# First mixer of a two-layer decoder trunk: tap rows and block sums move into the buffers of x, and twelve of thirty taps go by DMA

## The chip, the cores and the metric

The kernel runs on one core of one Trainium2 chip. The metric is the device time of one execution in microseconds; three executions of the kernel before took 2146.83, 2148.3 and 2149.0 us, median 2148.3.

## What is computed

The reference is a two-layer trunk on a sequence of 1024 positions with 1024 channels. Layer 0 is the part that the change touches:

```python
def even_mixer(h, w_in, sc_conv_w, cf_conv_w, cf_conv_b, cf_ln_g, cf_ln_b, w_out):
    z = h @ w_in
    sc_b, sc_c, sc_x, cf_a, cf_g = jnp.split(
        z, [SC_WIDTH, 2 * SC_WIDTH, 3 * SC_WIDTH, 3 * SC_WIDTH + CF_WIDTH], axis=-1)
    y_sc = sc_b * causal_dwconv(sc_c * sc_x, sc_conv_w)
    u = cf_a * jax.nn.sigmoid(cf_g)
    u = causal_dwconv(u, cf_conv_w) + cf_conv_b
    u = jax.nn.silu(layernorm(u, cf_ln_g, cf_ln_b))
    return jnp.concatenate([y_sc, u], axis=-1) @ w_out
...
        h = rmsnorm(x, mix_norm_g[layer])
        if layer % 2 == 0:
            x = x + even_mixer(h, ev_w_in[j], ev_sc_conv_w[j], ev_cf_conv_w[j], ev_cf_conv_b[j],
                               ev_cf_ln_g[j], ev_cf_ln_b[j], ev_w_out[j])
```

The Conformer convolution (cf) has 31 taps over 512 channels, the short convolution (sc) three. Each layer ends in a gated feed-forward block. Inputs and outputs are float32.

## The kernel before

Everything is held transposed: channels on the 128 partitions, the 1024 positions along the row. A tile of 128 x 1024 is one block of 128 channels; 512 channels are four blocks, j = 0 to 3. Each float32 operand of a matmul is split into a high and a low part, so a product of 1024 x 128 weights with the normalised input is 48 matmuls of 128 x 512 (`in_unit`, all issued at L229).

The first mixer (`mixer0`) runs twenty such products: for each cf block a value and a gate (pa0, pg0, pa1, ... pg3), then for each sc block three (pc, px, pb). A weight tile comes from HBM by `fetch` (L167, SP's queue, two buffers) and is split into its parts by a cast on ACT (L179) and a subtraction on DVE (L180). Products go to PSUM tiles `mm`, of which there are three, and DVE reads them out: for cf blocks L734 and L737 in `cf_evac`, with a sigmoid on ACT (L735) between them; for sc blocks L789, L793 and L800. A product starts when its weights are split and one of the three `mm` buffers has been read out.

In `cf_evac` the gated block is t and the convolution's sum u starts on ACT with the last tap and the bias (L739). The other 30 taps per block are of two kinds. Those in `taps` are one DVE instruction each, u += w * shifted t (L743, taps 10 to 30). Those in `ptaps` (taps 1 to 9) are a scaled, shifted copy that ACT writes (L754, L757), into one buffer of the sum `box["a"]` for tap 1 and into a row of the pool `e` (7 buffers) for the others, followed by a DMA from POOL's queue that adds the row to the sum (L758). At a block's end DVE adds that sum to u (L762). `run(6, 3)` between the products emits up to three `ptaps` and six `taps`.

A scheduler of the framework reorders what is emitted by its own model of the times; the order in which the instructions stand on each engine is then fixed. Each engine works its own list off in that order and stops at the first instruction whose inputs or buffers are not ready. What matters on ACT is that the casts, the sigmoids, the first sc tap (L795) and the tap rows share one list.

After the products, eight output tiles are formed, four per half of the sequence (`out_pair`, L400 adds them to x on DVE), while sums over channels for the layernorm are taken: L819 to L821 sum the four blocks, L829 and L832 square them on ACT, L833 adds the squares on POOL. Through all of this x itself, 4 MB, is resident in four slots of the pool `xpool` (`class X`, two slots for each half of the sequence); the mixer's in-projections need only its normalised copy.

Of the kernel before, what the change touches and what calls it, by code (L numbers as in the profile page):

```python
# [12 lines left out]
AF = mybir.ActivationFunctionType  # L13
ALU = mybir.AluOpType
# [4 lines left out]
S = 1024  # L19
NT = S // P  # L20
KD = D // P
# [21 lines left out]
U_EVIN, U_EVOUT = 0, 20  # L43
# [8 lines left out]
def trunk(ctx, tc, x, wpk, par, wgate, masks, ident, out):  # L52
    nc = tc.nc
# [11 lines left out]
    def nm(s):  # L65
        uid[0] += 1
        return f"{s}_{uid[0]}"
# [4 lines left out]
    def g_tile(dt=F32):  # L72
        return E["g"].tile([P, 1024], dt, tag="g", name=nm("g"))

    def x_tile(slot, a=4, b=512):
        return xpool.tile([P, a, b], F32, tag=f"x{slot}", name=nm("x"))
# [14 lines left out]
    def e_tile(dt=F32):  # L91
        return E["e"].tile([P, 1024], dt, tag="e", name=nm("e"))

    def mm_tile():
        return E["mm"].tile([P, 1024], F32, tag="mm", name=nm("mm"))
# [69 lines left out]
    def fetch(u):  # L165
        raw = raw_tile()
        nc.sync.dma_start(raw, wpk[u])  # L167
        return raw
# [7 lines left out]
    def split(raw, alloc, parts=(slice(0, 1024),)):  # L176
        hi, lo = w_pair() if alloc is None else (alloc(), alloc())
        for p in parts:
            nc.scalar.copy(hi[:, p], raw[:, p])  # L179
            last_lo[0] = nc.vector.tensor_sub(lo[:, p], raw[:, p], hi[:, p].bitcast(F32))  # L180
        return hi, lo

    def load_w(u, alloc=None):
        raw = raws.pop(u) if u in raws else fetch(u)
        return split(raw, alloc, cuts) if u == U_EVIN else split(raw, alloc)

    xs = [X(2 * hf) for hf in range(2)]
# [7 lines left out]
    for i in range(1, 8):  # L195
        hf, c = i // 4, 2 * (i % 4)
# [10 lines left out]
    def pc(name, i=0):  # L207
        c = _C[name] + i
        return parm[:, c:c + 1]
# [18 lines left out]
    def mm(o, l, r, st, sp):  # L228
        nc.tensor.matmul(o, lhsT=l, rhs=r, start=st, stop=sp)  # L229
# [12 lines left out]
    def diag(dg, rs, nt):  # L242
        for T in range(nt):
            nc.scalar.activation(dg[:, T * P:(T + 1) * P], idt, AF.Identity, scale=rs[:, T:T + 1])
# [126 lines left out]
    def in_first(units, norm, hooks):  # L371
        pss, ws = [], []
        for hf in range(2):
            for i, u in enumerate(units):
                if hf == 0:
                    ws.append(load_w(u))
                    pss.append(mm_tile())
                in_part(pss[i], ws[i], norm.hT, hf, lambda k: hooks.get((hf, i, k), lambda: None)())
        return pss

    def in_unit(u, hT):
        w = load_w(u)
        ps = mm_tile()
        in_full(ps, w, hT)
        return ps
# [16 lines left out]
    def conv_rest(t, src, ws, n):  # L402
        for j in range(1, n):
            nc.vector.scalar_tensor_tensor(t[:, j:], src[:, :S - j], ws(n - 1 - j), t[:, j:], ALU.mult, ALU.add)  # L404
# [319 lines left out]
        st.close()  # L724


    def mixer0(xs, norm, hooks):
        hT = norm.hT
        us, taps, ptaps = [], [], []
        NPT = 9  # L730

        def cf_evac(j, pa, pg):
            sg, t = e_tile(), g_tile()
            nc.vector.tensor_mul(sg, norm.br, pg)  # L734
            nc.scalar.activation(sg, sg, AF.Sigmoid)  # L735
            nc.vector.tensor_mul(sg, sg, norm.br)
            nc.vector.tensor_mul(t, sg, pa)  # L737
            u = e_tile()
            nc.scalar.activation(u, t, AF.Identity, bias=pc("cfb", j), scale=pc("cfw", 4 * 30 + j))  # L739
            us.append(u)  # L740

            def dve(s):
                return lambda: nc.vector.scalar_tensor_tensor(  # L743
                    u[:, s:], t[:, :S - s], pc("cfw", 4 * (30 - s) + j), u[:, s:], ALU.mult, ALU.add)

            box = {}

            def pool(s):
                def f():
                    w = pc("cfw", 4 * (30 - s) + j)  # L750
                    if s == 1:
                        box["a"] = g_tile()
                        nc.vector.memset(box["a"][:, 0:1], 0.0)
                        nc.scalar.activation(box["a"][:, 1:], t[:, :S - 1], AF.Identity, scale=w)  # L754
                    else:
                        tmp = e_tile()
                        nc.scalar.activation(tmp[:, s:], t[:, :S - s], AF.Identity, scale=w)  # L757
                        nc.gpsimd.dma_start(box["a"][:, s:], tmp[:, s:], accum_op=ALU.add)  # L758
                return f
            ptaps.extend(pool(s) for s in range(1, NPT + 1))  # L760
            taps.extend(dve(s) for s in range(NPT + 1, 31))
            taps.append(lambda: nc.vector.tensor_add(u, u, box["a"]))  # L762

        def run(n, m):
            for _ in range(min(m, len(ptaps))):
                ptaps.pop(0)()
            for _ in range(min(n, len(taps))):
                taps.pop(0)()

        cf = [U_EVIN + i for i in range(8)]  # L770
        pa0, pg0, pa1 = in_first(cf[:3], norm, hooks)
        cf_evac(0, pa0, pg0)
        run(6, 3)
        pg1 = in_unit(cf[3], hT)
        cf_evac(1, pa1, pg1)
        run(6, 3)
        for j in (2, 3):
            pa = in_unit(cf[2 * j], hT)
            run(6, 3)
            pg = in_unit(cf[2 * j + 1], hT)  # L780
            cf_evac(j, pa, pg)
            run(6, 3)

        ysc = []
        for j in range(4):
            u = U_EVIN + 8 + 3 * j
            pcv = in_unit(u, hT)
            c = e_tile()
            nc.vector.tensor_mul(c, norm.br, pcv)  # L789
            nc.vector.tensor_mul(c, c, norm.br)  # L790
            run(6, 3)
            px = in_unit(u + 1, hT)
            nc.vector.tensor_mul(c, c, px)  # L793
            t = e_tile()
            nc.scalar.activation(t, c, AF.Identity, scale=pc("scw", 8 + j))  # L795
            conv_rest(t, c, lambda i: pc("scw", 4 * i + j), 3)
            nc.vector.tensor_mul(t, t, norm.br)
            run(6, 3)
            pb = in_unit(u + 2, hT)
            nc.vector.tensor_mul(t, t, pb)  # L800
            ysc.append(split(t, r_tile))
            run(6, 3)
        run(1000, 1000)


        parts = [(ysc[k], load_w(U_EVOUT + k)) for k in range(4)]

        def out_sc(i):
            out_pair(xs, i // 4, i % 4, parts)

        def colsum(on, sm):
            ps = mm_tile()
            for hf in range(2):
                s = slice(hf * 512, (hf + 1) * 512)
                mm(ps[:, s], on, sm[:, s], True, True)
            return ps

        sm = e_tile()
        nc.gpsimd.tensor_add(sm, us[0], us[1])  # L819
        nc.gpsimd.tensor_add(sm, sm, us[2])  # L820
        nc.vector.tensor_add(sm, sm, us[3])  # L821
        out_sc(0)
        pm = colsum(one1, sm)
        sq = e_tile()
        for j in range(4):
            nc.vector.scalar_tensor_tensor(us[j], pm, -1.0 / 512.0, us[j], ALU.mult, ALU.add)
        for j in range(4):
            if j == 0:
                nc.scalar.activation(sq, us[j], AF.Square)  # L829
            else:  # L830
                s2 = e_tile()
                nc.scalar.activation(s2, us[j], AF.Square)  # L832
                nc.gpsimd.tensor_add(sq, sq, s2)  # L833
        for T in (1, 2, 3):
            out_sc(T)
        rs = colvec(sq, 8, 1.0 / 512.0)
        dg = e_tile()
        diag(dg, rs, 8)
        for T in (4, 5):
            out_sc(T)  # L840
        pr = colsum(one1, dg)
        vh, vl = rows4(), rows4()
        ycf = []
        for j in range(4):
            nc.vector.tensor_mul(us[j], us[j], pr)
            nc.scalar.activation(us[j], us[j], AF.Silu, bias=pc("lnb", j), scale=pc("lng", j))
            nc.scalar.copy(vh[j], us[j])
            nc.vector.tensor_sub(vl[j], us[j], vh[j].bitcast(F32))
            ycf.append((vh[j], vl[j]))
        for T in (6, 7):  # L850
            out_sc(T)
        return [(ycf[k], load_w(U_EVOUT + 4 + k)) for k in range(4)]


    def lru(norm):
# [452 lines left out]
    norm = Plain(0, xs)  # L1308
# [6 lines left out]
    def second():  # L1315
        norm.spread(0)
        for c in range(KD):
            norm.stat(1, c)

    parts = mixer0(xs, norm, {(0, 2, 4): lambda: norm.prep(0), (1, 0, 0): second,  # L1320
                              (1, 1, 4): lambda: norm.prep(1), (1, 2, 2): lambda: norm.spread(1)})

    ste.close()
# [21 lines left out]
    box = {}  # L1345
# [18 lines left out]
    norm = box["n"]  # L1364
# [8 lines left out]
    norm, early = attention(ys, norm, st)  # L1373
# [95 lines left out]
```

## Time and profile before

| | |
|---|---|
| median of three runs | 2148.3 us |
| profiled execution, its own time | 2147.01 us |
| its span, first to last instruction | 2145.2 us |
| PE busy | 2078.2 us, 97% |
| DVE busy | 1534.0 us, 72% |
| ACT busy | 915.5 us, 43% |
| POOL busy | 218.6 us, 10% |
| mean granted TensorE clock | 0.986 of full |
| chain that ended last | PE 68%, DVE 11%, DMA 10% of the span |

The profile is of one execution. Busy time counts an engine's own instructions, not its waits; a matmul's end is modelled, so PE's idle time tells more than its busy share. The trace gives for each idle stretch what ended it ("<-"). The first mixer lies between 0 and about 320 us of the span, the cf and sc products between 6 and 254 us.

### The profile page before, as it was taken

The numbers are of one execution on the slowest core, as the hardware profiler recorded it, in microseconds if no ns is written. First come the engines' busy times: TensorE is split into PE (matmuls) and PEld (weight loads), VectorE is DVE, ScalarE is ACT, GpSimd is POOL, SyncE is SP. The second block draws the span as 40 slices with busy tenths as digits, with TensorE's granted clock in tenths as the row PEclk, the third lists the DMA queues.
The fourth block names the chain that finished last, engine by engine and source line by source line (L and its number), as shares of the span: only waits on it lengthen the run. The fifth ranks groups of instructions, "written<-read, shape, count | busy, mean of one in ns | idle before, by whom it ended". The sixth has DMA issues, their size and how long they took to land.

```text
span 2145.2 us, 26963 instructions
## 1 busy us (share of the span) xinstructions
PE 2078.2 (97%) x10260; PEld 1741.1 (81%) x10260; DVE 1534.0 (72%) x2185; ACT 915.5 (43%) x1446; POOL 218.6 (10%) x209
## 2 busy tenths in 40 slices
PE   8997998999999999998999999999899999999999
PEld 6886886888888888787889999877688888888877
DVE  6987858878788777758595233585988787776764
ACT  6433335444444333436373444453544344443332
POOL 0111200000000000000044121220000000000000
PEclk9999998999999999999999999998899999999999
DMA  4566321344434478642212211232254443469643
GB/s 175 120 140 133 88 70 69 118 133 128 116 111 133 133 229 291 215 128 99 69 40 80 90 50 43 88 96 93 68 138 133 133 123 112 120 186 313 213 146 108
DMA packets 121202, 271.75 MB, mean 127 GB/s; under 512 B 12016, under 2 KB 20720, under 8 KB 121072
## 3 DMA queue, kind: packets, MB, share of 16 engines
q1 hardware_dynamic: 106672, 235.89, 33.3%
q0 software_dynamic: 14112, 33.99, 8.9%
q8 instruction: 80, 1.31, 0.3%
q14 instruction: 50, 0.41, 0.1%
q10 hardware_dynamic: 288, 0.15, 0.0%
HBM read 174.59 MB, written 78.71 MB: 118 GB/s over the span
## 4 chain that ended last, share of the span: by engine, by line
PE 68%; DVE 11%; DMA 10%; issue 2%; ACT 2%; POOL 0%; SPq 0%; DVEq 0%; ACTq 0%; POOLq 0%
PE u L461 38%; PE pq L229 8%; PE u L636 7%; PE mm L229 7%; DMA rd<-in_wpk_dram 4%; DMA g<-e 2%; PE S L229 2%; PE pl L229 2%; PE ud L636 2%; DMA rd<-fscr 1%; DVE x L914 1%; DMA hT<-in_wpk_dram 1%; DVE w L612 1%; DVE hT L283 1%; DVE x L641 1%
## 5 line engine op out<-in xcount | busy, mean ns | idle before, releaser
L461 PE MATMUL u<-hT,s 128*128 128x512 f32 x2016 | 481.7, 391 | 1.1 <-DVE s L453 1.0
L461 PEld LDWEIGHTS u<-hT,s 128*128 128x128 f32 x2016 | 379.0, 188 | 83.1 <-DVE s L453 1.9
L229 PE MATMUL mm<-hT,w 128*128 128x512 f32 x1536 | 364.0, 397 | 24.1 <-DVE e L800 9.4
L229 PEld LDWEIGHTS mm<-hT,w 128*128 128x128 f32 x1536 | 292.6, 191 | 91.7 <-issue 18.7
L461 PE MATMUL u<-w,s 128*128 128x512 f32 x1056 | 255.6, 390 | 1.4 <-ACT x L506 1.4
L461 PEld LDWEIGHTS u<-w,s 128*128 128x128 f32 x1056 | 198.6, 188 | 44.6 <-ACT x L506 1.8
L229 PE MATMUL pq<-w,hT 128*128 128x256 f32 x1728 | 223.3, 286 | 0.7 <-ACT k L996 0.5
L229 PEld LDWEIGHTS pq<-w,hT 128*128 128x128 f32 x1728 | 211.6, 191 | 3.8 <-issue 1.3
L636 PE MATMUL u<-w,w 128*128 128x512 f32 x616 | 184.0, 393 | 4.3 <-DVE w L612 4.3
L452 ACT CAST s<-ts 128x512 fp32r<-128x512 f32 x176 | 108.7, 620 | 138.0 <-PE u L461 130.2
L453 DVE TENSOR_TENSOR s<-ts,s 128x512 fp32r<-128x512 f32 x176 | 119.4, 687 | 55.9 <-ACT s L452 55.9
L461 PE MATMUL u<-hy,s 128*128 128x512 f32 x528 | 140.1, 408 | 11.5 <-DVE s L453 6.6
L636 PEld LDWEIGHTS u<-w,w 128*128 128x128 f32 x616 | 116.0, 189 | 30.0 <-DVE w L612 5.2
L461 PEld LDWEIGHTS u<-hy,s 128*128 128x128 f32 x528 | 102.4, 195 | 37.4 <-DVE s L453 8.0
L404 DVE SCALAR_TENSOR_TENSOR x<-x,parm,x 128x1023 f32<-128x1023 f32 x88 | 112.5, 1280 | 17.3 <-ACT x L489 15.2
L636 PE MATMUL u<-w 128*128 128x512 f32 x308 | 112.3, 390 | 0.0
L611 ACT CAST w<-rd 128x1024 fp32r<-128x1024 f32 x68 | 69.6, 1048 | 86.7 <-PE u L636 72.3
L180 DVE TENSOR_TENSOR w<-raw,w 128x1024 fp32r<-128x1024 f32 (+2 forms) x61 | 77.0, 1264 | 41.1 <-ACT w L179 40.9
L743 DVE SCALAR_TENSOR_TENSOR e<-g,parm,e 128x1010 f32<-128x1010 f32 (+20 forms) x84 | 102.2, 1256 | 1.9 <-ACT e L739 1.7
L179 ACT CAST w<-raw 128x1024 fp32r<-128x1024 f32 (+2 forms) x61 | 62.5, 1031 | 82.8 <-PE mm L229 43.8
L636 PE MATMUL u<-hy,hy 128*128 128x512 f32 x328 | 97.8, 392 | 0.0
L489 ACT ACTIVATE x<-x,parm 128x1024 f32<-128x1024 f32 x44 | 54.8, 1246 | 96.0 <-DVE x L488 96.0
(254 smaller groups left out, 3080.0 us busy)
## 6 DMA issues: line engine op xcount, KB each, us to landing
raw<-in_wpk_dram SPq DMA_DIRECT2D x103, 512.0 KB, 4.1
fscr<-x SPq DMA_DIRECT2D x154, 256.0 KB, 4.2
rd<-fscr SPq DMA_DIRECT2D x58, 512.0 KB, 4.6
r<-in_wpk_dram SPq DMA_DIRECT2D x44, 512.0 KB, 4.2
fscr<-x POOLq DMA_DIRECT2D x66, 256.0 KB, 8.1
xscr<-x SPq DMA_DIRECT2D x48, 256.0 KB, 2.3
x<-xscr SPq DMA_DIRECT2D x24, 512.0 KB, 6.5
hT<-in_wpk_dram SPq DMA_DIRECT2D x22, 512.0 KB, 8.3
```

Source lines behind the costliest of these rows:

```text
L179: nc.scalar.copy(hi[:, p], raw[:, p])
L180: last_lo[0] = nc.vector.tensor_sub(lo[:, p], raw[:, p], hi[:, p].bitcast(F32))
L229: nc.tensor.matmul(o, lhsT=l, rhs=r, start=st, stop=sp)
L283: nc.vector.scalar_tensor_tensor(lo, src, scale, hi.bitcast(F32), ALU.mult, ALU.subtract)
L404: nc.vector.scalar_tensor_tensor(t[:, j:], src[:, :S - j], ws(n - 1 - j), t[:, j:], ALU.mult, ALU.add)
L452: nc.scalar.copy(w[:, 0, :], self.s[name])
L453: nc.vector.tensor_sub(w[:, 1, :], self.s[name], w[:, 0, :].bitcast(F32))
L461: nc.tensor.matmul(bank, lhsT=l, rhs=r[:, k, :], start=first and k + j == 0, stop=k == 3 and j == 2, skip_group_check=True)
L489: nc.scalar.activation(t, g, AF.Identity, bias=pc(f"fb{layer}", f), scale=pc(f"fw{layer}", 44 + f))
L611: nc.scalar.copy(hi[:, c, :], src)
L636: nc.tensor.matmul(bank[m], lhsT=l[:, w, c], rhs=r[:, b, :], start=first and j == 0, stop=j == 2, skip_group_check=True)
L743: return lambda: nc.vector.scalar_tensor_tensor(u[:, s:], t[:, :S - s], pc("cfw", 4 * (30 - s) + j), u[:, s:], ALU.mult, ALU.add)
```

## The change

x is no longer kept: once its normalised copy exists, the four slots of `xpool` are given to the tap convolution, each as two rows of 1024. Slots 0 and 1 hold tap rows in turn (four rows in all), slots 2 and 3 hold two sums per block, for odd and even taps, blocks in turn. Twelve taps per block go by DMA instead of nine: taps 1 and 2 are written directly into the two sums (L763), taps 3 to 12 are rows (L766) that are added to the sum of their parity (L767), and after tap 12 one more DMA adds one sum to the other (L769). DVE keeps taps 13 to 30 (L750) and the final add (L773). The emission is `run(5, 3)` six times and then `deal`, which spreads what is left evenly. After the last product x is loaded again by eight DMAs on POOL's queue (L825). Five adds of the layernorm's sums move from POOL to DVE.

```diff
-    def mixer0(xs, norm, hooks):
+    def mixer0(norm, hooks):
...
-        NPT = 9
+        NPT = 12
+        rows = []
+
+        def tap_row():
+            if not rows:
+                t = x_tile(len(ptaps) // 2 % 2, 2, 1024)
+                rows.extend((t[:, 1, :], t[:, 0, :]))
+            return rows.pop()
...
                     if s == 1:
-                        box["a"] = g_tile()
-                        nc.vector.memset(box["a"][:, 0:1], 0.0)
-                        nc.scalar.activation(box["a"][:, 1:], t[:, :S - 1], AF.Identity, scale=w)
+                        box["a"] = x_tile(2 + j % 2, 2, 1024)
+                    a = box["a"][:, s % 2, :]
+                    if s <= 2:
+                        nc.vector.memset(a[:, 0:s], 0.0)
+                        nc.scalar.activation(a[:, s:], t[:, :S - s], AF.Identity, scale=w)
                     else:
-                        tmp = e_tile()
+                        tmp = tap_row()
                         nc.scalar.activation(tmp[:, s:], t[:, :S - s], AF.Identity, scale=w)
-                        nc.gpsimd.dma_start(box["a"][:, s:], tmp[:, s:], accum_op=ALU.add)
+                        nc.gpsimd.dma_start(a[:, s:], tmp[:, s:], accum_op=ALU.add)
+                    if s == NPT:
+                        nc.gpsimd.dma_start(box["a"][:, 1, :], box["a"][:, 0, :], accum_op=ALU.add)
...
-            taps.append(lambda: nc.vector.tensor_add(u, u, box["a"]))
+            taps.append(lambda: nc.vector.tensor_add(u, u, box["a"][:, 1, :]))
...
+        left = [12]
+
+        def deal():
+
+            n = left[0]
+            left[0] -= 1
+            run(-(-len(taps) // n), -(-len(ptaps) // max(n - 2, 1)))
...
-        run(1000, 1000)
+        xs = [X(0), X(2)]
+        for hf in range(2):
+            for c in range(0, KD, 2):
+                nc.gpsimd.dma_start(xs[hf].c(c, 2), x[hf, :, c:c + 2, :])
...
-        nc.gpsimd.tensor_add(sm, us[0], us[1])
-        nc.gpsimd.tensor_add(sm, sm, us[2])
+        nc.vector.tensor_add(sm, us[0], us[1])
+        nc.vector.tensor_add(sm, sm, us[2])
...
-                nc.gpsimd.tensor_add(sq, sq, s2)
+                nc.vector.tensor_add(sq, sq, s2)
```

The six `run(6, 3)` of the cf part become `run(5, 3)`, the twelve of the sc part `deal()`.

How the order moves is seen at three places. The first is POOL's list at the first block's accumulations, with the semaphores that each waits for; DMASW0, DMASW1 and so on are those of POOL's DMAs, given out in turn. Before (the sum is g_54_412):

```order
L758 DMA g_54_412<-e_55_415 128x1022 [waits Activation_49]
L758 DMA g_54_412<-e_56_418 128x1021 [waits DMASW0_49,Activation_49]
L758 DMA g_54_412<-e_63_489 128x1020 [waits DMASW1_49,Activation_49]
L758 DMA g_54_412<-e_64_492 128x1019 [waits DMASW2_49,Activation_49]
L758 DMA g_54_412<-e_65_495 128x1018 [waits DMASW3_49,Activation_49]
```

And now (the tile of both sums is x_54_412):

```order
L767 DMA x_54_412<-x_55_417 128x1020 [waits Activation_49]
L767 DMA x_54_412<-x_62_489 128x1019 [waits DMASW0_49,Activation_49]
L767 DMA x_54_412<-x_62_489 128x1018 [waits DMASW1_49,Activation_49]
L767 DMA x_54_412<-x_66_553 128x1017 [waits DMASW2_49,Activation_49]
L767 DMA x_54_412<-x_66_553 128x1016 [waits DMASW3_49,Activation_49]
L767 DMA x_54_412<-x_67_558 128x1015 [waits DMASW4_49,Activation_49]
L767 DMA x_54_412<-x_67_558 128x1014 [waits DMASW5_49,Activation_49]
L767 DMA x_54_412<-x_74_630 128x1013 [waits DMASW6_49,Activation_49]
L767 DMA x_54_412<-x_74_630 128x1012 [waits DMASW7_49,Activation_49]
L769 DMA x_54_412<-x_54_412 128x1024 [waits DMASW1_49,DMASW0_49]
```

Before, the second accumulation (128x1021) waited for the first, the third for the second. Now the second on the list (128x1020, the first row shown) waits for ACT alone, the third for the first, and so on, each for the one two places ahead; the joining DMA waits for both sums.

The second place is ACT's list up to the first sc activation. Before (e_781 to e_787 are rows of block 1, e_856 and e_859 the first of block 2):

```order
L757 ACTIVATE e_93_781<-g_61_482,parm_76 128x1017
L757 ACTIVATE e_94_784<-g_61_482,parm_76 128x1016
L757 ACTIVATE e_95_787<-g_61_482,parm_76 128x1015
L179 CAST w_133_1166<-raw_132_1164 128x1024
L757 ACTIVATE e_101_856<-g_76_628,parm_76 128x1022
L757 ACTIVATE e_102_859<-g_76_628,parm_76 128x1021
L179 CAST w_141_1240<-raw_140_1238 128x1024
L795 ACTIVATE e_106_923<-e_99_850,parm_76 128x1024
```

And now (x_121_1195 holds taps 11 and 12 of block 2; x_132_1336 and x_127_1267 are taps 5 and 6 and taps 3 and 4 of block 3; w_117_1136 are the weights of pb1):

```order
L766 ACTIVATE x_121_1195<-g_72_621,parm_76 128x1013
L766 ACTIVATE x_121_1195<-g_72_621,parm_76 128x1012
L766 ACTIVATE x_132_1336<-g_84_763,parm_76 128x1019
L766 ACTIVATE x_132_1336<-g_84_763,parm_76 128x1018
L766 ACTIVATE x_127_1267<-g_84_763,parm_76 128x1021
L766 ACTIVATE x_127_1267<-g_84_763,parm_76 128x1020
L179 CAST w_117_1136<-raw_116_1134 128x1024
L814 ACTIVATE e_96_906<-e_90_836,parm_76 128x1024
```

All rows of blocks 0 to 2 and four of block 3 now stand ahead of the sc activation, where 18 rows stood before. x_127_1267 uses the slot of x_121_1195.

The third place is DVE's list from the second sc tap of block 0 to the instruction that frees the `mm` buffer for pb1. Before, that was L800 (it reads pb0, mm_112_948):

```order
L404 SCALAR_TENSOR_TENSOR e_106_923<-e_99_850,parm_76,e_106_923 128x1022
L180 TENSOR_TENSOR w_145_1303<-raw_144_1301,w_145_1303 128x1024
L743 SCALAR_TENSOR_TENSOR e_77_633<-g_76_628,parm_76,e_77_633 128x1003
L743 SCALAR_TENSOR_TENSOR e_92_779<-g_91_774,parm_76,e_92_779 128x1008
L743 SCALAR_TENSOR_TENSOR e_62_487<-g_61_482,parm_76,e_62_487 128x994
L797 TENSOR_TENSOR e_106_923<-e_106_923,br_38_291 128x1024
L743 SCALAR_TENSOR_TENSOR e_77_633<-g_76_628,parm_76,e_77_633 128x1002
L743 SCALAR_TENSOR_TENSOR e_92_779<-g_91_774,parm_76,e_92_779 128x1007
L762 TENSOR_TENSOR e_62_487<-e_62_487,g_78_635 128x1024
L800 TENSOR_TENSOR e_106_923<-e_106_923,mm_112_948 128x1024
```

Now it is L808, which reads pc1 (mm_107_999); L819, which reads pb0, stands right behind it:

```order
L404 SCALAR_TENSOR_TENSOR e_96_906<-e_90_836,parm_76,e_96_906 128x1022
L180 TENSOR_TENSOR w_123_1207<-raw_122_1205,w_123_1207 128x1024
L750 SCALAR_TENSOR_TENSOR e_85_768<-g_84_763,parm_76,e_85_768 128x1007
L750 SCALAR_TENSOR_TENSOR e_73_626<-g_72_621,parm_76,e_73_626 128x1001
L773 TENSOR_TENSOR e_61_485<-e_61_485,x_78_695 128x1024
L816 TENSOR_TENSOR e_96_906<-e_96_906,br_38_291 128x1024
L750 SCALAR_TENSOR_TENSOR e_85_768<-g_84_763,parm_76,e_85_768 128x1006
L750 SCALAR_TENSOR_TENSOR e_73_626<-g_72_621,parm_76,e_73_626 128x1000
L762 MEMSET x_126_1262 128x1
L762 MEMSET x_126_1262 128x2
L808 TENSOR_TENSOR e_108_1048<-br_38_291,mm_107_999 128x1024
L819 TENSOR_TENSOR e_96_906<-e_96_906,mm_100_928 128x1024
```

Ahead of this piece now stand, from the L180 of pb1's weights on, three L750, the first L404 and three L750 more. One tap fewer stands between the second L404 and the read-out, and the buffer's release has moved from pb0's to pc1's read.

## Rows read from the trace of the kernel before

**Rows 1.** PE's timeline, 50 to 262 us: start, length, instructions, idle time before.
```profile
50.67 110.60 PE L229 MATMUL mm<-hT,w 128*128 128x512 f32 x480 [2.75 <-DVE e L734]
169.99 12.72 PE L229 MATMUL mm<-hT,w 128*128 128x512 f32 x48 [8.72 <-DVE e L800]
185.76 23.64 PE L229 MATMUL mm<-hT,w 128*128 128x512 f32 x96 [3.06 <-DVE e L789]
210.12 43.78 PE L229 MATMUL mm<-hT,w 128*128 128x512 f32 x192 [0.72 <-DVE e L800]
```

**Rows 2.** Busy time by stretch; the last three columns are clock, DMA share, GB/s.
```profile
160.00:180.00 20.00, 11.28 (x43) 8.95 (x42) 13.41 (x12) 6.09 (x6) 2.84 (x4) 0.83 0.70 153
180.00:200.00 20.00, 16.94 (x68) 13.50 (x68) 15.85 (x15) 7.99 (x8) 4.14 (x5) 0.91 0.56 105
```

**Rows 3.** Table of waits, 50 to 260 us: total, times, longest.
```profile
POOL g L758 <- DMA g<-e: 87.3, 18, 7.8
ACT e L757 <- DMA g<-e: 64.9, 17, 7.0
```

**Rows 4.** POOL's timeline, issues of accumulations.
```profile
58.15 1.07 POOL L758 DMA_DIRECT2D g<-e  x1 [16.56 <-ACT e L757]
...
131.26 0.87 POOL L758 DMA_DIRECT2D g<-e  x1 [4.23 <-DMA g<-e]
136.31 0.87 POOL L758 DMA_DIRECT2D g<-e  x1 [4.18 <-DMA g<-e]
...
149.75 0.87 POOL L758 DMA_DIRECT2D g<-e  x1 [6.47 <-DMA g<-e]
...
184.83 1.76 POOL L758 DMA_DIRECT2D g<-e  x2 [4.19 <-ACT e L757]
192.68 0.87 POOL L758 DMA_DIRECT2D g<-e  x1 [6.09 <-DMA g<-e]
```

**Rows 5.** Stretches around one pair of accumulations and one alone, columns as in rows 2.
```profile
184.80:186.10 1.30, 0.34 (x2) 0.32 (x3) 1.30 (x2) 0.00 (x0) 1.27 (x2) 1.00 0.00 0
186.10:191.70 5.60, 5.60 (x19) 4.43 (x18) 5.60 (x6) 1.15 (x1) 0.49 (x1) 0.70 0.99 186
137.60:140.40 2.80, 2.80 (x14) 2.33 (x13) 2.80 (x3) 0.00 (x0) 0.00 (x0) 1.00 0.99 186
```

**Rows 6.** DMA queues, 59 to 160 us: packets, MB, share; and the weight loads.
```profile
q0 software_dynamic: 2608, 9.46, 50.0%
q1 hardware_dynamic: 1152, 4.19, 13.8%
...
raw<-in_wpk_dram SPq DMA_DIRECT2D x8, 512.0 KB, 3.9
```

**Rows 7.** ACT's timeline, first tap rows and the first sc activation.
```profile
56.70 2.17 ACT L757 ACTIVATE e<-g,parm 128x1022 f32<-128x1022 f32 x2
...
149.32 1.15 ACT L795 ACTIVATE e<-e,parm 128x1024 f32<-128x1024 f32 x1 [1.20 <-DMA g<-e]
```

**Rows 8.** DVE's timeline, the run up to PE's release.
```profile
148.78 1.21 DVE L180 TENSOR_TENSOR w<-raw,w 128x1024 fp32r<-128x1024 f32 x1
...
168.63 1.21 DVE L800 TENSOR_TENSOR e<-e,mm 128x1024 f32<-128x1024 f32 x1
```

**Rows 9.** Groups of instructions, 50 to 260 us: busy and mean ns, idle before.
```profile
L743 DVE SCALAR_TENSOR_TENSOR e<-g,parm,e 128x1010 f32<-128x1010 f32 (+20 forms) x84 | 102.2, 1256 | 1.9 <-ACT e L739 1.7
...
L179 ACT CAST w<-raw 128x1024 fp32r<-128x1024 f32 x17 | 17.7, 1041 | 26.5 <-PE mm L229 26.5
...
L820 POOL TENSOR_TENSOR e<-e,e 128x1024 f32<-128x1024 f32 x1 | 3.3, 3270 | 0.1
L819 POOL TENSOR_TENSOR e<-e,e 128x1024 f32<-128x1024 f32 x1 | 2.4, 2390 | 12.2 <-DVE g L180 12.2
```

**Rows 10.** DVE's timeline, first residual adds.
```profile
264.29 1.21 DVE L400 TENSOR_TENSOR x<-x,mm 128x1024 f32<-128x1024 f32 x1
...
272.03 1.22 DVE L400 TENSOR_TENSOR x<-x,mm 128x1024 f32<-128x1024 f32 x1 [4.22 <-PE mm L229]
```

More of the change, by code (lines that the diff above doesn't have):

```diff
@@ L772, in mixer0 @@
         cf_evac(0, pa0, pg0)
-        run(6, 3)
+        run(5, 3)
         pg1 = in_unit(cf[3], hT)
         cf_evac(1, pa1, pg1)
-        run(6, 3)
+        run(5, 3)
         for j in (2, 3):
             pa = in_unit(cf[2 * j], hT)
-            run(6, 3)
+            run(5, 3)
             pg = in_unit(cf[2 * j + 1], hT)
             cf_evac(j, pa, pg)
-            run(6, 3)
+            run(5, 3)
+        left = [12]
[3 more added lines that the diff above has]
+            run(-(-len(taps) // n), -(-len(ptaps) // max(n - 2, 1)))
         ysc = []
@@ L790, in mixer0 @@
             nc.vector.tensor_mul(c, c, norm.br)
-            run(6, 3)
+            deal()
             px = in_unit(u + 1, hT)
@@ L797, in mixer0 @@
             nc.vector.tensor_mul(t, t, norm.br)
-            run(6, 3)
+            deal()
             pb = in_unit(u + 2, hT)
@@ L801, in mixer0 @@
             ysc.append(split(t, r_tile))
-            run(6, 3)
-        run(1000, 1000)
+            deal()
+        xs = [X(0), X(2)]
+        for hf in range(2):
+            for c in range(0, KD, 2):
+                nc.gpsimd.dma_start(xs[hf].c(c, 2), x[hf, :, c:c + 2, :])
         parts = [(ysc[k], load_w(U_EVOUT + k)) for k in range(4)]
@@ L851, in mixer0 @@
             out_sc(T)
-        return [(ycf[k], load_w(U_EVOUT + 4 + k)) for k in range(4)]
+        return xs, [(ycf[k], load_w(U_EVOUT + 4 + k)) for k in range(4)]
     def lru(norm):
@@ L1318, in second @@
             norm.stat(1, c)
-    parts = mixer0(xs, norm, {(0, 2, 4): lambda: norm.prep(0), (1, 0, 0): second,
+    xs, parts = mixer0(norm, {(0, 2, 4): lambda: norm.prep(0), (1, 0, 0): second,
                               (1, 1, 4): lambda: norm.prep(1), (1, 2, 2): lambda: norm.spread(1)})
```

## The prediction, made before the change was run

> **What bounds the kernel now.** I read the granted clock and PE's own timeline first, then the table of waits, then the queues that feed the wait. PE is busy 97% of the span, so what counts is where it stands still. Call the twenty in-projections of the first mixer products 1 to 20 (48 matmuls each; 12 is the first of short-conv block 1, 14 its last). PE runs products 4 to 13 without a gap, stands 8.72 us before product 14, 3.06 before 15 and 0.72 before 17 [rows 1]: three waits for DVE, 12.5 us. After the two long ones the granted clock of the stretch is 0.83 and 0.91 instead of 1.00, so a part of it ran at the lower level, 1.2 GHz [rows 2]. At full clock a product takes 43.78 / 4 = 10.95 us; product 14 took 12.72 and the pair 15 and 16 took 23.64, so each long stop cost about 1.8 us more [rows 1].
>
> Why is DVE late? It is not only full. ACT waits 64.9 us in that stretch for accumulations to land before it may write the next tap row, and POOL waits 87.3 us for the one before [rows 3]. ACT works in order, so the weight casts, the gate activations and the short conv's first tap stand behind those rows: ACT's first L795 started at 149.32, released by a DMA [rows 7], and DVE then worked off 18 instructions from the cast of 148.78 to the L800 of 168.63 that freed PE [rows 8]. The spacing of that run is (169.84 - 148.78) / 18 = 1.17 us, which I use for every DVE instruction here.
>
> **The transfers.** A lone accumulation is issued every 5.05 us (131.26, 136.31) [rows 4]. Of this 2.8 us is movement, during which the 16 engines are 0.99 busy at 186 GB/s, whether one runs (137.6 to 140.4) or two were issued together (186.1 to 191.7, 5.6 us) [rows 5]. So two in flight hide the 2.3 us around the movement (1.3 from issue to the first byte, 184.83 to 186.1; 1.0 from the last byte to the next issue, 191.7 to 192.68), but the movement itself does not overlap. The shares say the same: from 59 to 160 us queue q0 took 50.0% of the engines for 2608 / 144 = 18.1 accumulations, 2.79 us each, and q1 13.8% for 8 weight loads, 1.74 us each [rows 6].
>
> **The change, part by part.**
> *Tap instructions.* 12 of the 84 L743 go, 12 x 1.17 = 14.0 us less on DVE [rows 9]; two adds of L819 and L820 (2.39 and 3.27 us on POOL [rows 9]) and three squares' adds come to DVE, 5 x 1.17 = 5.9 us. Neither is on the path: DVE waits for ACT in the first stretch, and after 264.29 it idles 4.22 us before each residual add [rows 10]. If that cover were gone, the three adds would cost 3.5 us.
> *Accumulations.* 32 become 44 (per block ten rows and one that adds the two sums). The order on POOL shows each waiting for the one two before it, so two are in flight; the movement is 44 x 2.8 = 123 us instead of 90.
> *ACT's order is what decides.* In the order of before, ACT's first short-conv activation stands behind 18 accumulated tap rows; now it stands behind 34, and the last pair (block 3, taps 3 and 4) goes into the buffer of block 2's taps 11 and 12. It cannot be written before those two have landed, and they are numbers 31 and 32 on POOL's queue (11 + 11 + 10). Right behind it stands product 14's weight cast.
>
> So, with the trace's durations: the first accumulation was issued at 58.15 [rows 4]; now two rows are written directly instead of one, 1.1 us later (2.17 for two [rows 7]), 59.2; first byte at 60.5. 32 x 2.8 = 89.6 brings 150.1. Eight weight loads must pass on the same engines, 8 x 1.74 = 13.9: 164.0. Where a block's two sums are joined, the joining transfer waits for both and the queue pauses 2.3 us, twice before number 32; I let the loads fill these pauses (both ends below). Landed at 164.5; ACT writes two rows (2 x 1.1) and casts product 14's weights (1.04, the mean of L179 [rows 9]): 167.7. DVE has by then run into that cast; from L180 of these weights to L808 of product 12, which frees PE's buffer, stand 17 instructions and two small memsets: 17 x 1.17 = 19.9, so **187.6 for product 14, against 169.99** [rows 1]: +17.6. DVE's earlier stops, at gate activations behind tap rows, only move PE's idle time forward and are inside this number.
>
> From there PE sets the pace: seven products, 12.72 + 6 x 10.95 = 78.4, where before 169.99 to 253.90 took 83.9: -5.5. DVE needs 55 x 1.17 = 64 us for what stands up to the last L819, less than PE's 78. **Sum: +17.6 - 5.5 = +12.1 us.**
>
> *Reload of x.* Eight more transfers, 8 x 1.74 = 13.9 us of the engines, 8 x 0.9 of POOL issue. The slots of the tap rows are free once the last accumulation has landed, some 12 x 2.8 and the loads after 164, about 205; the first residual add, 264.29 before [rows 10], comes at about 276. 70 us cover 14: nothing. Without that cover it would be at most 13.9. The sums moved off POOL have no other user there: nothing.
>
> Profiled execution of before 2147.0 us (span 2145.2), so 2159.1; the median of the runs, 2148.3, lies 1.3 above it, and the prediction for a median is **2160 us**.
>
> *Bounds.* The unknown is how densely the queue runs with two in flight. At best loads and pauses cost nothing (number 32 moved at 150.1): 13.9 earlier, -1.8, 2146. At worst loads and both pauses count (4.6 more) and a transfer that meets another lingers, as the 6.47 us wait before 149.75 against 4.2 otherwise [rows 4] shows: 2.3 for three such meetings, 6.9: +23.6, 2172.
>
> **What the skill's rule would make of it.** Row: 2.8 us of movement for 0.5 MB, busy all through [rows 5]. The Trainium skill, "DMA: Bandwidth & Descriptors", section "Anatomy of one DMA — SWDGE (gpsimd) path", fits a transfer as about 2.0 us plus bytes over 436 GB/s, an estimate of 1.2 us of movement for one tap row. By that number 32 accumulations would not delay ACT and the first rival below would hold; the trace's 186 GB/s, for an accumulation that reads, adds and writes, speaks against it.
>
> **Rivals.**
> *The transfers keep up (faster).* If accumulations came at 2.4 us or less with everything between them, number 32 would have landed at 138.2, the cast would be done at 141.4 and L808 at 161.3, just where product 13 ended. PE then loses none of the waits and lower clocks: -(8.72 + 3.06 + 0.72) - 2 x 1.8 = -16.1, 2132. For it: DVE is 14 us lighter and the transfers are no longer a single chain of 5.05. Against: 2.8 us in both rows of movement [rows 5]. Chance 0.12 with all cases below 2144.
> *About even.* Loads and pauses cost little: the best bound, 2146, and up to five us above. Chance 0.16.
> *Still slower.* The worst bound, or tap rows late enough to hold other casts as well: 2167 and above. Chance 0.15. Here too belongs x arriving late.
> *It does not do what it says:* the two sums, halves of one tile, are ordered as one chain. Then number 32 would come at 59.2 + 32 x 5.05 = 221, +57, 2205. The order shows waits two back, so this is excluded but for 0.02.
> *Forecast:* 2152.6 to 2167, chance 0.55.
>
> **How the numbers follow.** A measurement of this kernel tells about 0.2%, 4.3 us, from no change: below 2144 is faster, above 2152.6 slower. Slower 0.55 + 0.15 + 0.02 = 0.72, same 0.16, faster 0.12. The range 2141 to 2172 leaves out most of the first rival and the tail above the worst bound, about 2 in 10.
>
> **What would show it.** Right: accumulations issued from POOL some 3.3 us apart in the first three blocks, movement at about 190 GB/s without long gaps; ACT's tap rows (L766) waiting for them; ACT's first L814 at 160 to 175 instead of 149; one PE wait of 12 to 22 us before product 14, released by DVE at L808, and a shorter one before product 9 or 10; no wait for x at L400; nothing changed after the mixer. Wrong: PE without a gap to product 20 (then the movement overlaps), or a wait at L400, or accumulations still 5 us apart.

## The result and the profile after

The changed kernel took **2160.95 us** in the median of four runs (2158.95 to 2163.36), the kernel before 2147.57 in four runs beside it (2145.03 to 2149.0): ratio 1.0066, 95% interval [1.0052, 1.0079]. That is 13.4 us slower; 2160.0 was predicted. The profiled execution took 2160.88 us, its span is 2159.1 us.

PE's timeline of the changed kernel, 50 to 290 us (start, length, instructions, idle time before and what ended it), answers to [rows 1]:

```profile
50.48 56.27 PE L229 MATMUL mm<-hT,w 128*128 128x512 f32 x240 [2.75 <-DVE e L741]
112.05 12.92 PE L229 MATMUL mm<-hT,w 128*128 128x512 f32 x48 [5.30 <-DVE g L744]
126.56 11.13 PE L229 MATMUL mm<-hT,w 128*128 128x512 f32 x48 [1.60 <-DVE e L741]
138.25 32.89 PE L229 MATMUL mm<-hT,w 128*128 128x512 f32 x144 [0.55 <-DVE g L744]
188.15 77.75 PE L229 MATMUL mm<-hT,w 128*128 128x512 f32 x336 [17.01 <-DVE e L808]
265.73 4.25 PE L229 MATMUL mm<-g,w 128*128 128x512 f32 x18
```

The three waits of before, ahead of products 14, 15 and 17, have become one of 17.01 us ahead of product 14; products 14 to 20 then run as one piece of 77.75 us. New are 5.30 us before product 9 and 1.60 before product 10. The out-projection starts at 265.73. In the kernel before it started at 253.75:

```profile
253.75 4.25 PE L229 MATMUL mm<-g,w 128*128 128x512 f32 x18
```

So 12 of the 13.4 us stand at the end of the last product. The out-projection behind it has the same stretches on PE. The last 1 to 2 us arise further back and can't be told from the spread: from the start of the out-projection to the last instruction it is 1891.5 us in the profile of before and 1893.4 now, and in two of the experiments below, which change nothing there, 1889.4 (ten taps) and 1894.8 (nine).

What the wait is made of, read backwards. First DVE, 168 to 188 us, columns as above; answers to [rows 8]:

```profile
168.09 1.23 DVE L180 TENSOR_TENSOR w<-raw,w 128x1024 fp32r<-128x1024 f32 x1 [7.92 <-ACT w L179]
169.23 3.60 DVE L750 SCALAR_TENSOR_TENSOR e<-g,parm,e 128x1009 f32<-128x1009 f32 x3
...
184.41 2.43 DVE L750 SCALAR_TENSOR_TENSOR e<-g,parm,e 128x1006 f32<-128x1006 f32 x2
186.78 1.22 DVE L808 TENSOR_TENSOR e<-br,mm 128x1024 f32<-128x1024 f32 x1
```

DVE stood still for 7.92 us until ACT had cast product 14's weights, then worked without a pause for 18.7 us up to L808, the instruction that empties PE's buffer. Now ACT, 158 to 169 us; answers to [rows 7]:

```profile
158.11 2.19 ACT L766 ACTIVATE x<-g,parm 128x1019 f32<-128x1019 f32 x2 [5.20 <-DMA x<-x]
164.93 2.19 ACT L766 ACTIVATE x<-g,parm 128x1021 f32<-128x1021 f32 x2 [4.63 <-DMA x<-x]
167.02 1.04 ACT L179 CAST w<-raw 128x1024 fp32r<-128x1024 f32 x1
167.96 1.15 ACT L814 ACTIVATE e<-e,parm 128x1024 f32<-128x1024 f32 x1
```

The cast itself takes 1.04 us. It stands behind a pair of tap rows that may be written only when a DMA has emptied their slots, at 164.93. POOL's timeline, where those transfers are issued, answers to [rows 4]:

```profile
66.10 0.87 POOL L767 DMA_DIRECT2D x<-x  x1 [5.09 <-DMA x<-x]
...
80.72 0.87 POOL L767 DMA_DIRECT2D x<-x  x1 [1.69 <-DMA x<-x]
83.52 0.87 POOL L767 DMA_DIRECT2D x<-x  x1 [1.93 <-DMA x<-x]
86.40 0.87 POOL L767 DMA_DIRECT2D x<-x  x1 [2.01 <-DMA x<-x]
92.62 0.87 POOL L769 DMA_DIRECT2D x<-x  x1 [5.35 <-DMA x<-x]
93.64 0.87 POOL L767 DMA_DIRECT2D x<-x  x1
94.68 0.87 POOL L767 DMA_DIRECT2D x<-x  x1 [0.17 <-issue]
...
158.53 0.87 POOL L767 DMA_DIRECT2D x<-x  x1 [2.17 <-DMA x<-x]
165.38 0.87 POOL L769 DMA_DIRECT2D x<-x  x1 [5.97 <-DMA x<-x]
```

Two in flight: an issue every 2.5 to 2.9 us in the steady parts, not every 5.05. The DMA queues of the changed kernel, 59 to 170 us (packets, MB, share of 16 engines), answer to [rows 6]:

```profile
q0 software_dynamic: 4752, 17.19, 84.9%
q1 hardware_dynamic: 864, 3.15, 7.3%
```

4752 / 144 = 33 accumulations; 0.849 x 111 / 33 = 2.86 us each, against 2.79 of before: with two in flight each still takes the engines for as long. 864 / 144 = 6 weight loads took 0.073 x 111 = 8.1 us, 1.35 us each. The stretches around the waits (busy time of PE, PEld, DVE, ACT, POOL, then granted clock, DMA share, GB/s), answering to [rows 2]:

```profile
100.00:120.00 20.00, 14.70 (x57) 11.74 (x56) 10.03 (x11) 9.57 (x9) 6.10 (x7) 0.83 1.02 202
140.00:160.00 20.00, 20.00 (x90) 16.57 (x89) 13.12 (x12) 10.28 (x10) 6.03 (x7) 1.00 1.03 205
180.00:200.00 20.00, 11.86 (x46) 9.70 (x47) 18.36 (x18) 6.73 (x7) 4.36 (x5) 0.73 0.80 170
```

The DMA engines are full while in the first two stretches DVE and ACT are busy only 9.6 to 13.1 us of 20. Lastly the waits, 50 to 265 us (total, times, longest), answering to [rows 3]:

```profile
POOL x L767 <- DMA x<-x: 69.2, 27, 5.1
ACT x L766 <- DMA x<-x: 64.2, 17, 8.7
DVE w L180 <- ACT w L179: 25.5, 5, 7.9
...
PE mm L229 <- DVE e L808: 17.0, 1, 17.0
...
ACT w L179 <- DMA raw<-in_wpk_dram: 1.6, 1, 1.6
```

ACT waits as long for DMA as before (64.2 against 64.9), though each transfer is issued sooner: there are more of them in the same list. DVE's wait for weight casts is new in this size (5.1 us before). The weights themselves are not late: in all this time ACT waited for a weight load once, for 1.6 us.

### The profile page after: what moved, and what is told of

Read it like the earlier page. It is cut to its first block, busy times and chain, and to the rows that moved or that the text cites. A ratio compares the mean times of both kernels' runs of the same rounds, so it can differ in the third digit from the quotient of the medians.

```text
span 2159.1 us, 26981 instructions
## 1 busy us (share of the span) xinstructions
PE 2079.2 (96%) x10260; PEld 1739.6 (81%) x10260; DVE 1522.9 (71%) x2182; ACT 927.8 (43%) x1458; POOL 221.2 (10%) x224
## 4 chain that ended last, share of the span: by engine, by line
PE 76%; DVE 11%; DMA 8%; issue 2%; ACT 2%; POOL 0%; SPq 0%; DVEq 0%; POOLq 0%; ACTq 0%
PE u L461 37%; PE mm L229 11%; PE u L636 10%; PE pq L229 8%; DMA x<-x 4%; DMA rd<-in_wpk_dram 3%; PE ud L636 3%; PE S L229 2%; PE pl L229 2%; DVE x L936 1%; DVE w L612 1%; DVE hT L283 1%; PE pa L229 1%; PE pt L1136 1%; DVE x L641 1%
## 5 line engine op out<-in xcount | busy, mean ns | idle before, releaser
L404 DVE SCALAR_TENSOR_TENSOR x<-x,parm,x 128x1023 f32<-128x1023 f32 (+1 forms) x88 | 112.7, 1281 | 17.3 <-ACT x L489 15.2
L180 DVE TENSOR_TENSOR w<-raw,w 128x1024 fp32r<-128x1024 f32 (+2 forms) x61 | 76.0, 1245 | 61.3 <-ACT w L179 61.0
L535 POOL DMA_DIRECT2D fscr<-x x22 | 19.2, 871 | 749.0 <-DVE x L531 746.1
```

## The experiments

Two theories stand against each other. **The list:** the transfers' pace decides when ACT gets past the tap rows that stand ahead of product 14's cast and first activation (L814, or L813 or L815 where lines are shifted), and that place decides the start of product 14. **Something else:** the number of transfers as such, DVE's extra adds, or the reload of x.

**Half the bytes.** Each of the 40 tap-row accumulations moves the second half of its columns only; the first half of the tap sums is left out. The four joins stay whole.

```diff
-                        nc.gpsimd.dma_start(a[:, s:], tmp[:, s:], accum_op=ALU.add)
+                        nc.gpsimd.dma_start(a[:, 512:], tmp[:, 512:], accum_op=ALU.add)
```

> Each of the 40 tap-row accumulations moves only the upper 512 of its 1024 columns (the lower half of every tap sum is left out of the DMA); their number, their waits, the ACT rows and the DVE work stay. Theory (the movement of the accumulations, 2.8 us each, sets when ACT reaches product 14's weight cast): movement falls to about 1.4 us, the accumulation ahead of that cast lands some 40 us earlier, PE's waits of 5.3, 1.6 and 17.0 us go with the two stretches at lower clock, about 28 us in all: 2133 us, +-4. Rival (the fixed time around a transfer, 2.3 us, or DVE's own instructions set L808): little changes, 2155 to 2161.

Measured: 2138.26 us (2134.04 to 2144.95), ratio to before 0.9969 [0.9953, 0.9985]. PE's timeline of this kernel:

```profile
131.35 32.91 PE L229 MATMUL mm<-hT,w 128*128 128x512 f32 x144 [3.04 <-DVE g L744]
166.89 78.03 PE L229 MATMUL mm<-hT,w 128*128 128x512 f32 x336 [2.63 <-DVE e L808]
```

The number of transfers is the same and so are the 34 accumulated rows ahead of the first L814, though the scheduler exchanged some neighbours in the lists of DVE, ACT and POOL. L814 stands at 146.96 in place of 167.96, released by DVE and not by a DMA, and product 14 starts 21 us sooner; the kernel is 23 us faster than the change. So it is the movement of the transfers, not their number, that costs the time. The forecast range ended at 2137: the waits of 3.04 and 2.63 us were not expected. Ahead of the second, DVE works without a stop from 135.25 to L808 at 165.53, so there DVE's own work is next.

**Rows emitted more slowly in the cf part.** Four lines of this kind:

```diff
-        run(5, 3)
+        run(5, 2)
```

By this edit a block's last addition (L773) comes ahead of that block's last tap rows in the order of emission, so the sums it adds to u lack these rows; the expectation did not see that.

> Same work, buffers and transfers as the change; only the emission is slower (two tap rows per run in the cf part instead of three, the rest dealt), so that 26 tap rows (20 of them accumulated) instead of 40 (34) stand ahead of the first short-conv activation on ACT. Theory (it is the place of rows in ACT's list): the 32nd accumulation no longer stands ahead of product 14's cast, PE's wait of 17.0 us goes, and the smaller ones with it: 2133 to 2140 us. Rival (the 44 transfers, the reload of x and the added DVE work cost the time wherever they stand): 2158 to 2163.

Measured: 2163.66 us (2163.42 to 2166.42), ratio 1.0089 [1.0072, 1.0106]: the forecast time missed by 23 us or more. PE's timeline of this kernel, and POOL's:

```profile
166.95 35.18 PE L229 MATMUL mm<-hT,w 128*128 128x512 f32 x144 [5.22 <-DVE e L808]
...
261.13 5.83 PE L229 MATMUL mm<-g,w 128*128 128x512 f32 x18 [8.59 <-DVE e L808]
271.65 3.75 PE L229 MATMUL mm<-e,one 128*128 128x512 f32 x4 [4.69 <-DVE e L843]
```

```profile
106.36 0.87 POOL L767 DMA_DIRECT2D x<-x  x1 [20.59 <-DVE e L773]
...
163.62 0.87 POOL L767 DMA_DIRECT2D x<-x  x1 [14.59 <-DVE e L773]
...
252.76 0.89 POOL L769 DMA_DIRECT2D x<-x  x1 [5.64 <-DMA x<-x]
```

The time lies 0.7 us above the range of the rival, by which 44 transfers cost the same wherever they stand. Half of the theory's expectation holds: L814 stood at 145.63 and product 14 at 166.95, since fewer rows were ahead. But the rows held back by L773 (20.59 and 14.59 us of an idle queue) came at the end, the last join at 252.76, and PE paid there. So the run does not price the place of the rows alone, and it does not refute this rival either. It shows what is late next: at 2.86 us each, 44 transfers take 126 us, and all of them have to end ahead of the last block's final addition.

**No joins.** DVE adds both sums, the four transfers of L769 go.

```diff
-                    if s == NPT:
-                        nc.gpsimd.dma_start(box["a"][:, 1, :], box["a"][:, 0, :], accum_op=ALU.add)
...
             taps.append(lambda: nc.vector.tensor_add(u, u, box["a"][:, 1, :]))
+            taps.append(lambda: nc.vector.tensor_add(u, u, box["a"][:, 0, :]))
```

> The DMA that joins a block's two sums is taken out and DVE adds both sums to u itself (one more add per block): 40 accumulations instead of 44, no pause of the queue at block ends. Theory: two joins (2 x 2.8) and two pauses (2 x 2.3, partly filled by weight loads) lie ahead of product 14's cast, one DVE add more lies behind it: product 14 some 5 to 9 us earlier, 2152 to 2156 us. Rival (the joins' waits are the cause of the slowdown): all 13 us gone, 2148 or less. Rival (joins ride along free): 2160 to 2163.

Measured: 2159.8 us (2159.28 to 2160.28), ratio 1.0071 [1.0056, 1.0086]; product 14 at 187.92. A miss by some 4 us: two transfers fewer ahead of L813, which stood at 167.78, gave nothing. The rival that the joins ride along free (2160 to 2163) comes out, 0.2 us below its range. POOL's timeline of this kernel, where the first join was:

```profile
86.25 0.87 POOL L767 DMA_DIRECT2D x<-x  x1 [1.99 <-DMA x<-x]
94.11 0.87 POOL L767 DMA_DIRECT2D x<-x  x1 [6.99 <-ACT x L766]
```

From 86.25 to the next tap row's issue, 94.11, it is 7.9 us; in the change it was 86.40 to 93.64, 7.2 us, with the join inside. At the second border it was 10.3 us without the join (119.96 to 130.28) and 8.2 with it (121.12 to 129.36). At a block's border the next rows are not written yet, so the queue stands anyway. The joins ride in that gap.

**The five additions back on POOL** (two of L841 and L842, three of L855).

```diff
-        nc.vector.tensor_add(sm, us[0], us[1])
-        nc.vector.tensor_add(sm, sm, us[2])
+        nc.gpsimd.tensor_add(sm, us[0], us[1])
+        nc.gpsimd.tensor_add(sm, sm, us[2])
...
-                nc.vector.tensor_add(sq, sq, s2)
+                nc.gpsimd.tensor_add(sq, sq, s2)
```

> The five adds of the layernorm's sums go back from DVE to POOL, all else as in the change. Theory (they lie under cover on either engine): 2159 to 2163 us, no change. Rival (they hold DVE on the path): 3 to 6 us faster, 2155 to 2158.

Measured: 2159.46 us (2158.71 to 2170.47), ratio 1.0082 [1.0057, 1.0106]. Product 14 started at 188.84 after 17.40 us. No difference in the median: the additions cost nothing on either engine. The profiled execution was the slowest of the four, 2170.47; its out-projection starts at 267.92, 2.2 us later than in the change, and the rest of its excess lies behind the mixer.

**Eleven, ten, nine taps.** The number of tap rows was then the dose, with everything else as in the change. Odd counts need a counter of their own for the two row tiles:

```diff
-        NPT = 12
-        rows = []
+        NPT = 9
+        rows, turn = [], [0]
...
-                t = x_tile(len(ptaps) // 2 % 2, 2, 1024)
+                t = x_tile(turn[0], 2, 1024)
+                turn[0] ^= 1
```

> Eleven taps of a block in its two sums in place of twelve (the row slots keep alternating); the rest as in the change. The theory: product 14 starts when the tap rows ahead of its activation on ACT have found free slots, plus the 3 us of ACT and the 19 us of DVE behind them. With eleven, 30 accumulated rows stand ahead of the first L814 in place of 34, so the last pair there waits for transfer 28 in place of 32: 4 x 2.86 = 11.4 us earlier. L814 at 156 to 158, product 14 at 176 to 178 (188.15 in the changed kernel), its wait 5 to 7 us; time 2147 to 2152 against 2161. The rival, that the time goes by the number of transfers over the whole mixer (44 in the change at +13.4 us, 32 in the kernel before, 1.1 us each): 2155 to 2158.

> Ten taps of a block in its two sums. The theory: 28 accumulated rows ahead of the first L814, the last pair waits for transfer 26: 6 x 2.86 = 17.2 us earlier, so product 14's operand is ready at about 171, where PE ends product 13: a wait of 0 to 3 us; the wait of 5.30 before product 9 or 10 shrinks too. Time 2137 to 2144. The rival by the number of transfers (36): 2150 to 2154.

> Nine taps of a block in its two sums, as many as the kernel before sums by DMA in its one sum (32 transfers, four of them joins, against 32 before). The theory: 24 accumulated rows ahead of the first L814, transfer 22 frees the last pair at about 136: no wait before product 14, and none over 2 us elsewhere, so PE goes through the mixer as in the halved run: 2131 to 2139, faster than the kernel before. The rival by the number of transfers: as the kernel before, 2145 to 2150.

Measured, beside 2146.44 for the kernel before (the row of twelve is the measurement above):

| taps by DMA | accumulated rows ahead of the first L814 / L815 | that activation | product 14 | its wait | median us | ratio to before |
|---|---|---|---|---|---|---|
| 12 (the change) | 34 | 167.96 | 188.15 | 17.01 | 2160.95 | 1.0066 [1.0052, 1.0079] |
| 11 | 30 | 159.42 | 180.80 | 11.73 | 2151.15 | 1.0021 [1.0008, 1.0034] |
| 10 | 28 | 153.32 | 170.36 | 2.85 | 2144.24 | 0.9992 [0.9977, 1.0007] |
| 9 | 24 | 149.46 | 166.39 | 0.93 | 2137.17 | 0.9953 [0.9939, 0.9966] |

PE's timelines of the kernels with eleven and ten taps at product 14, then that of nine:

```profile
180.80 78.19 PE L229 MATMUL mm<-hT,w 128*128 128x512 f32 x336 [11.73 <-DVE e L809]
```

```profile
170.36 79.33 PE L229 MATMUL mm<-hT,w 128*128 128x512 f32 x336 [2.85 <-DVE e L809]
```

```profile
108.84 11.13 PE L229 MATMUL mm<-hT,w 128*128 128x512 f32 x48 [2.34 <-DVE g L745]
121.68 43.78 PE L229 MATMUL mm<-hT,w 128*128 128x512 f32 x192 [1.70 <-DVE e L742]
166.39 76.44 PE L229 MATMUL mm<-hT,w 128*128 128x512 f32 x336 [0.93 <-DVE e L809]
```

The fewer rows stand ahead on ACT, the sooner product 14 starts, and the time follows; the rival (1.1 us per transfer: 2155 to 2158, 2150 to 2154, 2145 to 2150) misses all three. A price of some 2 us per transfer would fit this series too (9.8, 6.9 and 7.1 us for four transfers each); the halved bytes, with all 44 transfers at 2138, exclude it. The activation of the table is on the path with twelve and eleven taps only. With ten, DVE comes to the instruction behind it at 156.11, after its end at 154.46, and has worked without a stop since 142.11; its last two stops, 2.73 us at 136.79 and 0.61 us, were for a weight cast and a cf activation behind other tap rows. With nine, its last stop is 1.51 us for product 14's cast, at 145.15. Several numbers fell short. With eleven taps L815 came 8.5 us sooner, not 11.4, so product 14 came at 180.80 and not at 176 to 178, after a wait of 11.73 us and not of 5 to 7. With nine, one wait is 2.34 us where none over 2 was expected, and ten taps ended 0.24 us above its range. Nine taps are **faster than both kernels**: 9 us under the kernel before, measured beside it, with 32 transfers like it. Which part of the change gives these 9 us was not tried apart.

**x reloaded twice.**

```diff
-        for hf in range(2):
-            for c in range(0, KD, 2):
-                nc.gpsimd.dma_start(xs[hf].c(c, 2), x[hf, :, c:c + 2, :])
+        for _ in range(2):
+            for hf in range(2):
+                for c in range(0, KD, 2):
+                    nc.gpsimd.dma_start(xs[hf].c(c, 2), x[hf, :, c:c + 2, :])
```

> The changed kernel with the eight transfers that reload x made twice. The theory: the reload lies under the products, the first add into x (L400) is at 277 and does not wait for x now; eight more transfers of about 3 to 4 us end at 265 to 275: no difference, 2159 to 2164. The rival, that the reload costs part of the time: one more costs it again, 2164 to 2175.

Measured: 2160.76 us (2160.01 to 2163.99), ratio 1.0067 [1.0042, 1.0092]. DVE's timeline of this kernel at the first residual addition:

```profile
277.65 1.22 DVE L400 TENSOR_TENSOR x<-x,mm 128x1024 f32<-128x1024 f32 x1
```

No wait stands ahead of it (277.41 in the change): the reload is under its cover with room for a second one.

**Below nine.** Eight taps (NPT = 8 in the edit above), and nine without the joins.

> Eight taps of a block in its two sums. With nine, the waits of PE in the mixer are down to 2.75, 2.34, 1.70 and 0.93 us and DVE is busy for the whole of 160 to 220 us, so the transfers no longer bound and DVE is next. The theory that DVE is then the limit: four more taps on DVE, 4 x 1.17 = 4.7 us, of which half or more comes back as waits of PE: 2137 to 2143. The rival, that fewer transfers go on paying: 2130 to 2135.

> Nine taps of a block in its two sums, without the joins by DMA: DVE adds both sums (four more additions of 1.17 us on it, 28 transfers in place of 32). If DVE is the limit with nine taps: as with nine or up to 5 us slower, 2136 to 2142. The rival, that the transfers still bound: 2130 to 2135.

Measured beside 2145.51 for before: eight taps 2139.79 us (2133.23 to 2145.35), ratio 0.997 [0.9957, 0.9983]; nine without joins 2136.27 (2134.46 to 2140.33), ratio 0.9967 [0.9952, 0.9982]. Neither gains on nine taps with joins (0.9953 [0.9939, 0.9966]). The intervals overlap, so no order among the three is shown. Both times lie in the range of the theory that DVE is then the limit (2137 to 2143, 2136 to 2142), and 2130 to 2135 is missed. The traces bear this theory out in part only. A stretch of the kernel with nine taps and the same of that with eight, columns as above:

```profile
160.00:180.00 20.00, 19.07 (x85) 15.48 (x84) 20.00 (x19) 2.00 (x2) 0.00 (x0) 1.00 0.08 27
```

```profile
160.00:180.00 20.00, 16.74 (x63) 13.65 (x64) 20.00 (x18) 3.49 (x4) 0.00 (x0) 0.83 0.17 52
```

DVE is busy for the whole 20 us and the DMA engines for 0.08 and 0.17 of them: in this stretch DVE sets the pace. But what stands ahead of it is not a full DVE alone. With eight taps PE is free for product 14 at 159.3 and waits 4.00 us for L809; DVE had stood 4.48 us for the first L815 (first line), which stands on ACT behind a pair of rows that had waited 5.40 us for a DMA (second line). Nine taps without joins show the same on DVE (third line), ahead of a wait of PE of 4.91 us:

```profile
150.18 1.28 DVE L404 SCALAR_TENSOR_TENSOR e<-e,parm,e 128x1023 f32<-128x1023 f32 x1 [4.48 <-ACT e L815]
```

```profile
146.91 2.19 ACT L767 ACTIVATE x<-g,parm 128x1019 f32<-128x1019 f32 x2 [5.40 <-DMA x<-x]
```

```profile
151.89 1.29 DVE L404 SCALAR_TENSOR_TENSOR e<-e,parm,e 128x1023 f32<-128x1023 f32 x1 [4.57 <-ACT e L814]
```

So the transfers still hold product 14 in both, though not by their pace alone. With eight taps POOL had issued none for 20.25 us up to 125.24, until ACT had written the next block's first rows (L764); ahead of these ACT had stood 6.96 us for DVE's final addition of an earlier block (L774), which frees the buffer of the sums. That DVE and the queue hold each other up in this way is read from the traces; no run took it away.

## Why the prediction was right, step by step

- **Pace of the transfers: right.** Movement of 2.8 us that does not overlap, with the 2.3 us around it hidden by two in flight: 2.86 us per transfer, issues 2.5 to 2.9 us apart. The spacing of "some 3.3 us", averaged over loads, fits too: from the issue at 66.10 to that at 158.53 there are 29 more, 3.2 us each. The best bound, where loads and pauses cost nothing, had the slot free at 150.1; it came at 164.93. The estimate of 1.2 us per row from the Trainium skill ("DMA: Bandwidth & Descriptors", section "Anatomy of one DMA — SWDGE (gpsimd) path") is excluded by the 2.86. The half-bytes run shows what a shorter movement would have given: 2138, near the first rival's 2132.
- **Number 32's landing: right to 0.4 us, by luck in part.** 164.5 forecast, rows written into its slot from 164.93. From the first issue at 59.0 that is 105.9 us. The forecast has 89.6 of movement, 13.9 of eight loads, nothing for pauses, and 0.5 from the last byte to the landing. Measured are 91.5 (32 x 2.86) and 8.1 for loads, as only six passed, at 1.35 us each and not 1.74; the engines stood for some 3 us between the first byte and the last, and another 2 us went by from the last byte, at about 162.8, to ACT's row. Loads sized 6 us too large cancel with the other three.
- **ACT's order decides: right.** Cast done at 167.7 forecast, 168.06 measured; the rows, the cast, DVE's list and PE's wait follow one another without a gap in the trace, and the halved bytes and the taps series move ACT's rows and product 14 together.
- **DVE behind the cast: right.** 17 instructions of 1.17 us, 19.9 us forecast from the start of L180 to the end of L808; measured 168.09 to 188.00, 19.9. With eleven taps it is one instruction more, 159.56 to 180.66, 21.1.
- **Product 14: 187.6 forecast, 188.15 measured,** 0.4 us from the cast and 0.2 behind L808.
- **Seven products from there: 78.4 forecast, 77.75 measured.** The lower clock took about 1.1 us (77.75 - 7 x 10.95), not 1.8. This error and that of product 14's start cancel.
- **The pauses at the joins:** the sum let loads fill them; a bound held 4.6 us against them. The run without joins shows that the queue pauses there anyway, because the new block's rows are not written yet, and that joins in this place are free. So the total was right, but not for the reason it gave.
- **Costed at nothing: right.** Additions back on POOL: no difference. Reload of x: no difference even when doubled, though its cover was smaller than the forecast's 70 us: the slots came free later, and the last two reloads were issued at 238.69, 39 us ahead of the first L400. The three taps a block that no longer run on DVE left it more time to wait: 25.5 us for weight casts alone.
- **Sum:** +12.1 forecast, +12 at the out-projection, +13.4 in the medians.
- **A slip in a rival:** with one chain, number 32 at 221 is 57 us behind the forecast's 164.0 and not behind the kernel before, so by the prediction's own terms that case is some 2217 us and not 2205. Nothing else rests on it.

What stays open is the place of the rows alone, with twelve taps kept and every row summed: the slower emission was meant for that and brought a wait of its own. The taps series changes place and number together, and the halved bytes keep both and change the movement; together they exclude a cost by number alone. They do not part the place of the rows from the total of the movement.

## What to carry to other kernels

Work that goes from a busy engine to DMAs is not free: price each transfer by its own movement, count how many stand ahead of the next critical instruction on the in-order engine that feeds them, and compare the sum with the time that the consumer has. Here, deepening the chain of transfers from one to two in flight hid only what lies around the movement; once the DMA engines showed a share of 1.0, more transfers only lengthened the queue. Look for the number by trying it: with nine taps by DMA and twenty-one on DVE the changed kernel is 0.5% faster than the kernel before, with twelve 0.7% slower, and with eight nothing more is gained. A time inside a theory's range is not yet the theory: with eight taps the trace still shows DVE waiting for a row.

## What the runs showed of the hardware

What a wait of PE cost afterwards at the clock did not go by its length. Seven products take 76.65 us at the full 2.4 GHz (7 x 10.95). Each number is from one execution: behind 0.93 us of idle time they took 76.44 (nine taps), behind 2.63 us 78.03 (halved bytes), behind 2.85 us 79.33 (ten taps), behind 4.00 us 78.79 (eight taps), behind 11.73 us 78.19 (eleven taps), behind 17.01 us 77.75 (the change), behind 17.40 us 79.24 (additions on POOL). A stretch of the kernel with ten taps, then two of the change, columns as above:

```profile
170.40:176.00 5.60, 5.60 (x13) 4.38 (x14) 5.60 (x6) 1.15 (x2) 0.00 (x0) 0.50 0.30 94
```

```profile
174.00:188.00 14.00, 0.00 (x0) 0.00 (x0) 14.00 (x16) 3.12 (x3) 1.74 (x2) 0.50 0.26 65
188.20:190.80 2.60, 2.60 (x6) 2.06 (x7) 2.60 (x3) 1.05 (x1) 0.87 (x1) 0.50 1.07 201
```

A clock of 0.50 is the lower level, 1.2 GHz. With ten taps PE worked at it from the end of its short wait on, for these 5.6 us and a little more (0.87 from 176 to 178, then 1.00). In the change the clock was there while PE stood still, and it was full again some 3 us after product 14 had begun (0.77 from 190 to 192, then 1.00). So the long wait of 17.01 us cost 1.1 us behind it and the short one of 2.85 us cost 2.7. What decides between the two was not tried.
